# Products of single column tiles in other orders: a two-layer decoder trunk on one core

## The chip, the cores and the metric

The kernel runs on one core of one Trainium2 chip. The metric is the device time of one execution in microseconds (us); less is better. PE is the matmul engine, PEld its weight loads, DVE, ACT and POOL the vector, scalar and gpsimd engines, SP the engine that issues most transfers.

## The reference

A decoder trunk of two layers for 256 tokens of width 1024. Each layer has an attention mixer and a gated feed-forward with a causal convolution of width 3 on the gate branch; a last RMS norm ends it. The change lies in the feed-forward:

```python
def conv_ffn(h, w_in, conv_w, conv_b, w_out):
    u, g = jnp.split(h @ w_in, 2, axis=-1)
    g = lax.conv_general_dilated(g, conv_w[:, None, :], window_strides=(1,),
                                 padding=[(CONV_WIDTH - 1, 0)],
                                 dimension_numbers=('NWC', 'WIO', 'NWC'),
                                 feature_group_count=D_FF) + conv_b
    return (jax.nn.gelu(g, approximate=False) * u) @ w_out
...
    for layer in range(DEPTH):
...
        h = h + conv_ffn(rmsnorm(h, ffn_norm[layer]), ffn_w_in[layer], ffn_conv_w[layer],
                         ffn_conv_b[layer], ffn_w_out[layer])
    return rmsnorm(h, final_norm)
```

Here `h` is 256 by 1024, `w_in` 1024 by 5632 (2816 columns for u, 2816 for g) and `w_out` 2816 by 1024.

## The kernel before

Every float32 operand of a large product is held as two parts, a high part and the rest (`whi` and `wlo` of a weight, `xs[:, k, 0]` and `xs[:, k, 1]` of the activation). A product is three matmuls added into one PSUM region: high times high (hh), high weight times low activation (hl), low weight times high activation (lh). Weights come in chunks of 128 by 2048 in the order of a list (`PLAN`); ACT copies a chunk's high part (L145) and DVE subtracts it (L146), in two pieces of 1024 columns.

A feed-forward works through 22 column tiles `f` of 128 of the 2816. In a product of a tile, u (`i` = 0) and g (`i` = 1) each add up over eight blocks `k` of 128 of the width. The two banks are `pd`. Tiles 0 to 4 take the dense form (`colmajor`, three matmuls of 256 columns per block; u and g are the two halves of one bank, and change after every trio). Tiles 5 to 21 (`NARROW` = 5) take the wide form (`product`): one matmul of 512 columns gives hh and hl side by side in the two halves of a bank, a second of 256 columns adds lh to the first half. `read_out` then adds the halves: ACT copies the low half to `lowp` (L876), DVE adds it (L877). DVE scales u and g into `gbuf` (L900), ACT and DVE do the convolution, ACT the gelu, POOL the gating, ACT and DVE split the result into the parts `o`.

Four tiles later (`LAGF` = 4) `proj` multiplies `o` with two rows of blocks of `w_out` and adds into banks that stay open through the whole feed-forward (`acc`). In layer 0 (`proj_tile`) these are four banks, each with two 256-column regions `c`, and the weight is the stationary operand: 24 matmuls of 256 columns per tile, hh, hl, lh for each `c`. In layer 1 (`final`, `proj_tail`) the activation is the stationary operand and the weights stream: five regions in five banks (`TAIL`), 15 matmuls per tile.

PE's order is the program's order. On the other engines the order in this loop is written out by hand too: product of `f`, split of a chunk if `f` is even, gelu and split of `f-1`, read-out of `f`, split of the next chunk with the convolution, then `proj(f-4)`. PSUM has eight banks, shared by `acc` and `pd`.

Of the kernel before, what the change touches and what calls it, by code (L numbers as in the profile page):

```python
# [28 lines left out]
S = 256  # L29
D = 1024  # L30
KD = D // 128
# [19 lines left out]
TAIL = ((0, 0, 512), (0, 512, 1024), (1, 0, 512), (1, 512, 768), (1, 768, 1024))  # L51
# [50 lines left out]
def trunk(ctx, tc, x, rel_bias, small, lam_p, wpack, fin_g, onehot, addrow, tab, out):  # L102
    nc = tc.nc
# [11 lines left out]
    def bank(name="ps"):  # L115
        return psum.tile([128, 512], F32, name=name, tag="ps")

    def t2(name, dt=F32, shape=(128, 2, S)):
        return two.tile(list(shape), dt, name=name, tag="t2")

    def mm(o, l, r, start, stop):
        nc.tensor.matmul(o, l, r, start=start, stop=stop, skip_group_check=True)  # L122
# [83 lines left out]
    xs = xpool.tile([128, KD, 2, S], F32R, name="xs")  # L206
# [243 lines left out]
        return kt, [((('qn', h), ('kn', h), 'kr'), stage_s), ((), stage_t), (('vm',), stage_o)]  # L450


    def proj_tile(acc, o, w, kk, first, last):
        oh, ol = o
        hi, lo = w
        for c in range(KD):
            a = acc[c // 2][:, (c % 2) * S:(c % 2 + 1) * S]
            s = slice(c * 128, (c + 1) * 128)
            mm(a, hi[:, kk, s], oh, first and c % 2 == 0, False)
            mm(a, hi[:, kk, s], ol, False, False)  # L460
            mm(a, lo[:, kk, s], oh, False, last)

    def close_phase(acc, g0):
        for j in range(4):
# [26 lines left out]
    def bc2(t):  # L491
        return t[:, None, :].to_broadcast([128, 2, S])
# [52 lines left out]
    def proj_units(prefix, order, store):  # L545
        box = {}

        def unit(i):
            kt = order[i]

            def run():
                if i == 0:
                    box['acc'] = [bank("acc") for _ in range(4)]
                proj_tile(box['acc'], store[kt], need(f"{prefix}{kt // 2}"), kt % 2, i == 0, i == KD - 1)
            return kt, run
        return [unit(i) for i in range(KD)], box
# [181 lines left out]
    def ffn(l, final):  # L738
        env, acts, box = {}, {}, {}
# [5 lines left out]
        def conv(f):  # L745
            g = gbuf[f % 3][:, 1]
            t1 = work.tile([128, S], F32, name="t1", tag="sc")
            nc.scalar.activation(t1, g[:, 2:], AF.Identity, bias=col(f, 3), scale=col(f, 2))  # L748
            return t1

        def taps(f, t1):
            g = gbuf[f % 3][:, 1]
            t3 = work.tile([128, S], F32, name="t3", tag="pt", bufs=6)
            nc.vector.scalar_tensor_tensor(t3, g[:, 1:S + 1], col(f, 1), t1, op0=ALU.mult, op1=ALU.add)
            nc.vector.scalar_tensor_tensor(t3, g[:, 0:S], col(f, 0), t3, op0=ALU.mult, op1=ALU.add)
            return t3

        def gelu(f, t3):
            ge = work.tile([128, S], F32, name="ge", tag="ex", bufs=6)
            nc.scalar.activation(ge, t3, AF.Gelu)  # L760
            nc.gpsimd.tensor_tensor(ge, ge, gbuf[f % 3][:, 0, 2:], op=ALU.mult)  # L761
            return ge

        def act_split(f, ge):
            o = t2("o", F32R)
            nc.scalar.activation(o[:, 0], ge, AF.Copy)  # L766
            nc.vector.tensor_tensor(o[:, 1], ge, o[:, 0].bitcast(F32), op=ALU.subtract)  # L767
            acts[f] = (o[:, 0], o[:, 1])
# [15 lines left out]
        def weights(f):  # L784
            n = f"f{l}o{f // 2}"
            return need(n) if f < NARROW - LAGF or f >= NF - LAGF else chunks[n]

        def proj(f):
            w = weights(f)
            first, last = f == 0, f == NF - 1  # L790
            if first:
                box['acc'] = [bank("acc") for _ in range(len(TAIL) if final else 4)]
            if not final:
                proj_tile(box['acc'], acts[f], w, f % 2, first, last)
                return
            for i in range(len(TAIL)):
                proj_tail(f, i)

        def proj_tail(f, i):
            w = weights(f)  # L800
            (oh, ol), (hi, lo) = acts[f], w
            tb, c0, c1 = TAIL[i]
            a = box['acc'][i][:, :c1 - c0]
            s = slice(tb * 128, (tb + 1) * 128)
            mm(a, oh[:, s], hi[:, f % 2, c0:c1], f == 0, False)
            mm(a, ol[:, s], hi[:, f % 2, c0:c1], False, False)
            mm(a, oh[:, s], lo[:, f % 2, c0:c1], False, f == NF - 1)
# [28 lines left out]
        for f in range(3, NARROW):  # L836
            dense(f)
            if final:
                hn_tile()
                hn_tile()  # L840
            if f >= LAGF:
                proj(f - LAGF)
# [8 lines left out]
        def next_chunk():  # L851

            i = split_at[0]
            if i >= len(PLAN):
                return [lambda: None] * 2
            split_at[0] += 1
            ps = pieces(i)[1]

            def step(n):
                if n == 0:  # L860
                    open_split(i)
                if n < len(ps):
                    split_piece(i, ps[n])
                if n == 1:
                    load_next()
            return [lambda: step(0), lambda: step(1)]

        def product(f, i, p):
            hi, lo = chunks[f"f{l}i{f}"]
            for k in range(KD):  # L870
                mm(p, hi[:, 8 * i + k], xs[:, k], k == 0, False)
                mm(p[:, :S], lo[:, 8 * i + k], xs[:, k, 0], False, k == KD - 1)

        def read_out(t, i, p):
            lowp = work.tile([128, S], F32, name="lowp", tag="ex", bufs=6)
            nc.scalar.activation(lowp, p[:, S:], AF.Copy)  # L876
            nc.vector.tensor_tensor(t[:, i], p[:, :S], lowp, op=ALU.add)  # L877

        need(f"f{l}i{NARROW}")
        with tc.manual_schedule(engines={mybir.EngineType.Activation, mybir.EngineType.DVE,  # L880
                                         mybir.EngineType.Pool, mybir.EngineType.SP}):
            t3 = None
            for f in range(NARROW, NF):
                even = f % 2 == 0
                pu, pg = bank("pd"), bank("pd")
                product(f, 0, pu)
                product(f, 1, pg)
                if even:
                    c = next_chunk()
                    c[0]()  # L890
                if t3 is not None:
                    ge = gelu(f - 1, t3)
                if even:
                    c[1]()
                if t3 is not None:
                    act_split(f - 1, ge)
                ug = t2("ug")
                read_out(ug, 0, pu)
                read_out(ug, 1, pg)
                nc.vector.tensor_tensor(gbuf[f % 3][:, :, 2:], ug, bc2(env['r_bc']), op=ALU.mult)  # L900
                c = next_chunk()
                c[0]()
                t3 = taps(f, conv(f))
                c[1]()
                proj(f - LAGF)
            act_split(NF - 1, gelu(NF - 1, t3))
        if not final:
            for f in range(NF - LAGF, NF):
                proj(f)
            close_phase(box['acc'], NORM1[1])  # L910
            return
# [3 lines left out]
        def piece(t, tb, c0, c1):  # L915
            return t[2 * tb + c0 // 512][:, c0 % 512:c0 % 512 + c1 - c0]

        for i, (tb, c0, c1) in enumerate(TAIL):
            for f in range(NF - LAGF, NF):
                proj_tail(f, i)  # L920
            h, o = piece(hn, tb, c0, c1), piece(y, tb, c0, c1)
            q = i if tb == 0 else i - 2
            nc.vector.tensor_add(h, box['acc'][i][:, :c1 - c0], h)
            t = t2("fsq", shape=(128, c1 - c0))
# [6 lines left out]
            if c1 == D:  # L931
# [4 lines left out]
                for c in range(2):  # L936
                    o = y[2 * tb + c]
# [17 lines left out]
    first = [bank("pd"), bank("pd")]  # L955
# [30 lines left out]
    split_at[0] = 3  # L986
    even_layer()
    ffn(0, False)
    odd_layer()
    ffn(1, True)  # L990


# [68 lines left out]
```

## Time and profile before

| what | value |
|---|---|
| median of 3 runs | 606.71 us (605.46 to 606.84) |
| profiled execution, its time | 607.95 us |
| its span, first to last instruction | 606.1 us |
| PE busy | 591.7 us, 98% of the span, 4078 matmuls |
| PE weight loads | 4078 |
| DVE busy / ACT busy / POOL busy | 73% / 58% / 17% |
| granted PE clock, mean over the span | 0.993 |

The span is the profiled execution's time on the core; its own time has 1.85 us more around it. Matmuls overlap in the pipe, so PE's busy time is not the sum of separate matmuls; how fast they follow each other is read from the starts in the timeline and from the chain of work that ended last.

### The profile page before, as it was taken

How to read it: one execution, taken by the hardware profiler on the slowest of the kernel's cores; microseconds unless marked ns; L12 is line 12 of the kernel's file. 1: busy time of each engine (PE TensorE's matmuls, PEld its weight loads, DVE VectorE, ACT ScalarE, POOL GpSimd, SP SyncE). 2: the span in 40 equal slices, each digit the busy share in tenths (PEclk: the TensorE clock that was granted, in tenths of full speed). 3: DMA queues.
4: the chain of work that ended last, by engine and by line, in shares of the span. 5: the costliest groups of instructions: out<-in, count | busy, mean ns of one | idle time of the engine just before them, and what ended most of it. 6: DMA issues, size and time to landing. Idle time of an engine off the chain costs nothing.

```text
span 606.1 us, 10380 instructions
## 1 busy us (share of the span) xinstructions
PE 591.7 (98%) x4078; PEld 544.6 (90%) x4078; DVE 443.0 (73%) x778; ACT 351.6 (58%) x647; POOL 103.0 (17%) x97
## 2 busy tenths in 40 slices
PE   8998999999999999999999999999989999999995
PEld 7887989999999999999999998999978888888884
DVE  5698757679877778777786975558857787777754
ACT  6558557466655556565564755645655565655633
POOL 4701122041101111001144101004201111011110
PEclk8999999999999999999999999999989999999999
DMA  7988543435455554554435343454535545554301
GB/s 264 335 322 316 193 171 142 141 138 208 146 203 209 209 183 169 203 207 166 170 120 215 134 147 132 144 196 119 202 140 208 198 164 195 209 176 170 142 0 70
DMA packets 19961, 108.77 MB, mean 179 GB/s; under 512 B 2430, under 2 KB 5448, under 8 KB 7752
## 3 DMA queue, kind: packets, MB, share of 16 engines
q1 hardware_dynamic: 16416, 104.17, 47.4%
q10 hardware_dynamic: 3336, 3.41, 1.7%
q0 software_dynamic: 160, 0.52, 0.4%
q8 instruction: 32, 0.52, 0.4%
q14 instruction: 17, 0.14, 0.1%
HBM read 107.02 MB, written 1.08 MB: 178 GB/s over the span
## 4 chain that ended last, share of the span: by engine, by line
PE 84%; DVE 6%; DMA 4%; ACT 2%; issue 1%; POOL 1%; SPq 0%; POOLq 0%; ACTq 0%; DVEq 0%
PE pd L122 48%; PE acc L122 26%; PE pv L122 4%; DMA raw<-in_wpack_dram 3%; DVE wlo L146 3%; PE pO L122 2%; PE pS L122 2%; DMA hT<-in_x_dram 1%; PE puq L122 1%; DVE ex L341 1%; DVE sc L331 1%; ACT whi L145 1%; PE pukv L122 0%; POOL ge L761 0%; PE pT L345 0%
## 5 line engine op out<-in xcount | busy, mean ns | idle before, releaser
L122 PE MATMUL pd<-xs,whi 128*128 128x256 f32 (+1 forms) x1312 | 331.3, 332 | 3.7 <-ACT hn L833 2.2
L122 PE MATMUL pd<-xs,wlo 128*128 128x256 f32 x928 | 258.0, 283 | 0.4 <-DVE wlo L146 0.4
L146 DVE TENSOR_TENSOR wlo<-raw,whi 128x1024 fp32r<-128x1024 f32 (+1 forms) x183 | 229.3, 1278 | 26.4 <-ACT whi L145 26.2
L122 PEld LDWEIGHTS pd<-xs,whi 128*128 128x128 f32 x1312 | 221.0, 191 | 27.1 <-ACT whi L145 2.5
L145 ACT ACTIVATE whi<-raw 128x1024 fp32r<-128x1024 f32 (+1 forms) x195 | 196.4, 1032 | 69.4 <-PE pd L122 18.2
L122 PEld LDWEIGHTS pd<-xs,wlo 128*128 128x128 f32 x928 | 175.7, 192 | 0.8 <-DVE wlo L146 0.8
L122 PE MATMUL acc<-o,whi 128*128 128x256 f32 x608 | 108.7, 281 | 0.0
L122 PEld LDWEIGHTS acc<-o,whi 128*128 128x128 f32 x608 | 92.7, 188 | 1.0 <-issue 0.2
L761 POOL TENSOR_TENSOR ge<-ge,gbuf 128x256 f32<-128x256 f32 x44 | 37.4, 851 | 294.8 <-ACT ge L760 294.8
L122 PE MATMUL acc<-o,wlo 128*128 128x256 f32 x304 | 84.7, 279 | 0.0
L876 ACT ACTIVATE lowp<-pd 128x256 f32<-128x256 f32 x68 | 25.9, 381 | 81.2 <-PE pd L122 81.1
L877 DVE TENSOR_TENSOR ug<-pd,lowp 128x256 f32<-128x256 f32 x68 | 28.5, 419 | 52.7 <-ACT lowp L876 52.7
L122 PE MATMUL acc<-whi,o 128*128 128x512 f32 (+1 forms) x220 | 58.5, 351 | 0.2 <-ACT o L766 0.2
L122 PEld LDWEIGHTS acc<-o,wlo 128*128 128x128 f32 x304 | 57.2, 188 | 0.0
L122 PEld LDWEIGHTS acc<-whi,o 128*128 128x128 f32 x220 | 38.6, 189 | 7.5 <-ACT o L766 0.7
L146 POOL TENSOR_TENSOR wlo<-raw,whi 128x1024 fp32r<-128x1024 f32 (+1 forms) x12 | 26.3, 2192 | 104.2 <-ACT whi L145 58.0
L122 PE MATMUL acc<-wlo,o 128*128 128x512 f32 (+1 forms) x110 | 38.6, 351 | 0.0
L767 DVE TENSOR_TENSOR o<-ge,o 128x256 fp32r<-128x256 f32 x44 | 19.0, 438 | 22.1 <-ACT o L766 22.1
L748 ACT ACTIVATE t<-gbuf,ccol 128x256 f32<-128x256 f32 x44 | 26.4, 601 | 12.0 <-DVE gbuf L900 10.1
L766 ACT ACTIVATE o<-ge 128x256 fp32r<-128x256 f32 x44 | 18.4, 418 | 24.0 <-POOL ge L761 24.0
L334 ACT ACTIVATE ex<-sc,nm 128x256 f32<-128x256 f32 (+1 forms) x56 | 24.8, 444 | 9.6 <-DVE nm L331 9.4
L122 PE MATMUL pv<-whi,xs 128*128 128x512 f32 x96 | 30.2, 395 | 0.0
(152 smaller groups left out, 536.5 us busy)
## 6 DMA issues: line engine op xcount, KB each, us to landing
raw<-in_wpack_dram SPq DMA_DIRECT2D x95, 1024.0 KB, 4.8
raw<-in_wpack_dram SPq DMA_DIRECT2D x8, 256.0 KB, 4.6
Tt<-btab ACTq DMA_DIRECT2D x2, 1024.0 KB, 9.2
hT<-in_x_dram SPq DMA_DIRECT2D x4, 256.0 KB, 5.1
Tt<-btab ACTq DMA_DIRECT2D x1, 512.0 KB
raw<-in_wpack_dram SPq DMA_DIRECT2D x1, 512.0 KB
fin<-in_fin_g_dram POOLq DMA_DIRECT2D x2, 256.0 KB, 4.0
out_dram<-y SPq DMA_DIRECT2D x2, 256.0 KB, 2.0
```

Source lines behind the costliest of these rows:

```text
L122: nc.tensor.matmul(o, l, r, start=start, stop=stop, skip_group_check=True)
L145: nc.scalar.activation(hi[:, s], raw[:, s], AF.Copy)
L146: (eng or nc.vector).tensor_tensor(lo[:, s], raw[:, s], hi[:, s].bitcast(F32), op=ALU.subtract)
L331: nc.vector.tensor_tensor_reduce(out=t[:, a:b], in0=p[:, a:b], in1=rev(T, b - a), scale=-1.0, scalar=BIG, op0=ALU.add, op1=ALU.min, accum_ ...
L334: nc.scalar.activation(e[:, a:b], t[:, a:b], AF.Exp, bias=nm[:, i:i + 1], scale=-1.0, accum_out=den[:, i:i + 1])
L341: nc.vector.tensor_scalar(e[:, a:b], e[:, a:b], rd[:, i:i + 1], None, op0=ALU.mult)
L748: nc.scalar.activation(t1, g[:, 2:], AF.Identity, bias=col(f, 3), scale=col(f, 2))
L761: nc.gpsimd.tensor_tensor(ge, ge, gbuf[f % 3][:, 0, 2:], op=ALU.mult)
L766: nc.scalar.activation(o[:, 0], ge, AF.Copy)
L767: nc.vector.tensor_tensor(o[:, 1], ge, o[:, 0].bitcast(F32), op=ALU.subtract)
L876: nc.scalar.activation(lowp, p[:, S:], AF.Copy)
L877: nc.vector.tensor_tensor(t[:, i], p[:, :S], lowp, op=ALU.add)
```

## The change

In layer 0, tiles 5 to 9 keep the wide form with its two matmuls per block, in another order for tiles 6, 7 and 8. Tiles 10 to 16 leave the wide form for three matmuls of 256 columns into one half bank, in seven different orders. For them `read_out` is one DVE copy per bank and `lowp` is gone. The output products of tiles 5 to 9 in layer 0 go through their 24 matmuls in five other orders. In layer 1 only the output products of tiles 6 and 7 change their order; all else there is as before.

```diff
-    def proj_tile(acc, o, w, kk, first, last):
+    def proj_tile(acc, o, w, kk, first, last, order='triple'):
         oh, ol = o
         hi, lo = w
-        for c in range(KD):
+        three = ('hh', 'hl', 'lh')
+        seq = {'triple': [(c, x) for c in range(KD) for x in three],
+               'banks': [(c, x) for c in (0, 2, 4, 6, 1, 3, 5, 7) for x in three],
+               'pairs': [(c + i, x) for c in range(0, KD, 2) for x in three for i in range(2)],
+               'passes': [(c, x) for x in three for c in (0, 2, 4, 6, 1, 3, 5, 7)],
+               'hlh': [(c, x) for c in range(KD) for x in ('hh', 'lh', 'hl')],
+               'across': [(c + i, x) for c in (0, 1, 4, 5) for x in three for i in (0, 2)]}[order]
+        for c, x in seq:
...
+                order = {5: 'banks', 6: 'pairs', 7: 'passes', 8: 'hlh', 9: 'across'}.get(f, 'triple')
...
+            for tb in range(2) if f in (6, 7) else ():
+                (oh, ol), (hi, lo) = acts[f], w
+                s = slice(tb * 128, (tb + 1) * 128)
+                its = [(box['acc'][i][:, :c1 - c0], slice(c0, c1)) for i, (t, c0, c1) in enumerate(TAIL) if t == tb]
+                for a, c in its:
+                    if f == 6:
+                        mm(a, oh[:, s], hi[:, f % 2, c], False, False)
+                    else:
+                        mm(a, oh[:, s], hi[:, f % 2, c], False, False)
+                        mm(a, oh[:, s], lo[:, f % 2, c], False, False)
+                for a, c in its:
+                    mm(a, ol[:, s], hi[:, f % 2, c], False, False)
+                for a, c in its if f == 6 else ():
+                    mm(a, oh[:, s], lo[:, f % 2, c], False, False)
...
-        def product(f, i, p):
+        WIDE = {5: 'kpair', 6: 'kswap', 7: 'passes', 8: 'ug', 9: 'kpair'}
+        NARROW3 = {10: 'triple', 11: 'passes', 12: 'ug', 13: 'hlh', 14: 'lhh', 15: 'ugtriple', 16: 'ugk'}
+
+        def products(f, ps):
...
+            total = KD * (3 if f in NARROW3 and not final else 2)
...
+            order = 'kpair' if final else WIDE.get(f) or NARROW3.get(f) or 'kpair'
+            if total == 2 * KD:
+                seq = {'kpair': [(i, k, w) for i in range(2) for k in range(KD) for w in ('wide', 'lh')],
+                       'kswap': [(i, k, w) for i in range(2) for k in range(KD)
+                                 for w in (('wide', 'lh') if k % 2 == 0 else ('lh', 'wide'))],
+                       'passes': [(i, k, w) for i in range(2) for w in ('wide', 'lh') for k in range(KD)],
+                       'ug': [(i, k, w) for k in range(KD) for w in ('wide', 'lh') for i in range(2)]}[order]
+            else:
+                three, rot = ('hh', 'hl', 'lh'), ('hh', 'lh', 'hl')
+                seq = {'triple': [(i, k, w) for i in range(2) for k in range(KD) for w in three],
+                       'passes': [(i, k, w) for i in range(2) for w in three for k in range(KD)],
+                       'ug': [(i, k, w) for k in range(KD) for w in three for i in range(2)],
+                       'hlh': [(i, k, w) for i in range(2) for k in range(KD) for w in rot],
+                       'lhh': [(i, k, w) for i in range(2) for k in range(KD) for w in ('lh', 'hl', 'hh')],
+                       'ugtriple': [(i, k, w) for k in range(KD) for i in range(2) for w in three],
+                       'ugk': [(i, k, w) for w in three for k in range(KD) for i in range(2)]}[order]
...
+        def read_out(t, i, p, f):
+            if f in NARROW3 and not final:
+                nc.vector.tensor_copy(t[:, i], p[:, :S])
+                return
             lowp = work.tile([128, S], F32, name="lowp", tag="ex", bufs=6)
             nc.scalar.activation(lowp, p[:, S:], AF.Copy)
             nc.vector.tensor_tensor(t[:, i], p[:, :S], lowp, op=ALU.add)
```

PE, the start of the product of tile 10 of layer 0, before the change (`pd` are u's and g's banks, `whi` and `wlo` the parts of the weight, `xs` the activation):

```order
L122 MATMUL pd<-xs,whi 128x512
L122 MATMUL pd<-xs,wlo 128x256
L122 MATMUL pd<-xs,whi 128x512
L122 MATMUL pd<-xs,wlo 128x256
L122 MATMUL pd<-xs,whi 128x512
```

The same place with the change:

```order
L122 MATMUL pd<-xs,whi 128x256 x2
L122 MATMUL pd<-xs,wlo 128x256
L122 MATMUL pd<-xs,whi 128x256 x2
L122 MATMUL pd<-xs,wlo 128x256
L122 MATMUL pd<-xs,whi 128x256 x2
```

Each 512-column matmul has become two of 256, so a tile has 48 matmuls and 48 weight loads where it had 32 of each.

PE with the change, from tile 11's product (`passes`) over the output product of tile 7 (`acc`, `passes`) into tile 12's product (`ug`):

```order
L122 MATMUL pd<-xs,whi 128x256 x16
L122 MATMUL pd<-xs,wlo 128x256 x8
L122 MATMUL pd<-xs,whi 128x256 x16
L122 MATMUL pd<-xs,wlo 128x256 x8
L122 MATMUL acc<-o,whi 128x256 x16
L122 MATMUL acc<-o,wlo 128x256 x8
L122 MATMUL pd<-xs,whi 128x256 x4
L122 MATMUL pd<-xs,wlo 128x256 x2
```

Before, tile 11 was 16 pairs of 512 and 256 columns and the output product eight trios, and u was finished before g began; now the kinds stand in blocks, and in tile 12 u and g alternate after every matmul, so that both banks are finished only at the end.

DVE, the read-out of one of the tiles 10 to 16, before the change (`ug` is the tile that is scaled into `gbuf`, `wlo` the split of a weight chunk):

```order
L877 TENSOR_TENSOR ug<-pd,lowp 128x256 x2
L900 TENSOR_TENSOR gbuf_122<-ug,r_bc 128x2x256
L146 TENSOR_TENSOR wlo<-raw,whi 128x1024
L754 SCALAR_TENSOR_TENSOR t_2880<-gbuf_122,ccol_308,t_2878 128x256
L755 SCALAR_TENSOR_TENSOR t_2880<-gbuf_122,ccol_308,t_2880 128x256
```

The same place with the change:

```order
L926 COPY ug<-pd 128x256 x2
L952 TENSOR_TENSOR gbuf_122<-ug,r_bc 128x2x256
L146 TENSOR_TENSOR wlo<-raw,whi 128x1024
L760 SCALAR_TENSOR_TENSOR t_2952<-gbuf_122,ccol_308,t_2950 128x256
L761 SCALAR_TENSOR_TENSOR t_2952<-gbuf_122,ccol_308,t_2952 128x256
```

The two additions have become two copies, which no longer come after ACT's `lowp`; the rows around them stand in the same order.

## Rows read from the trace of the kernel before

**Rows 1.** The page's busy time, share of the span and instructions of each engine.

```profile
PE 591.7 (98%) x4078; PEld 544.6 (90%) x4078; DVE 443.0 (73%) x778; ACT 351.6 (58%) x647; POOL 103.0 (17%) x97
```

**Rows 2.** Chain that ended last, 120 to 320 us: start, us, what.

```profile
122.45 11.52 PE pd L122 x96
...
140.59 11.51 PE pd L122 x96
152.10 2.83 PE acc L122 x24
...
163.40 5.56 PE pd L122 x32
168.96 2.83 PE acc L122 x24
171.78 5.55 PE pd L122 x32
...
196.92 5.55 PE pd L122 x32
...
247.20 5.55 PE pd L122 x32
...
294.66 14.13 PE acc L122 x120
```

**Rows 3.** Busy time of each engine in two stretches (feed-forward loops of the two layers).

```profile
152.00:294.70 142.70, 142.70 (x955) 131.36 (x955) 107.69 (x154) 82.19 (x136) 15.20 (x18) 1.00 0.53 191
...
446.70:590.00 143.30, 143.28 (x792) 124.60 (x792) 103.96 (x149) 80.11 (x134) 14.07 (x17) 0.99 0.44 159
```

**Rows 4.** Timeline of PE at the program's start, by-kind order of matmuls.

```profile
17.06 1.12 PE L122 MATMUL pd<-xs,wlo 128*128 128x256 f32 x8
18.02 2.08 PE L122 MATMUL pd<-xs,whi 128*128 128x256 f32 x16
19.94 1.12 PE L122 MATMUL pd<-xs,wlo 128*128 128x256 f32 x8
20.90 0.40 PE L122 MATMUL pd<-xs,whi 128*128 128x256 f32 x2
```

**Rows 5.** Timeline of PE and PEld at 160 us: an output product of layer 0.

```profile
160.66 0.28 PE L122 MATMUL acc<-o,wlo 128*128 128x256 f32 x1
...
160.78 0.40 PE L122 MATMUL acc<-o,whi 128*128 128x256 f32 x2
160.90 0.19 PEld L122 LDWEIGHTS acc<-o,wlo 128*128 128x128 f32 x1
...
161.01 0.28 PE L122 MATMUL acc<-o,wlo 128*128 128x256 f32 x1
...
161.13 0.40 PE L122 MATMUL acc<-o,whi 128*128 128x256 f32 x2
```

**Rows 6.** Timeline of DVE after one product of layer 0.

```profile
161.10 0.43 DVE L877 TENSOR_TENSOR ug<-pd,lowp 128x256 f32<-128x256 f32 x1 [0.85 <-ACT lowp L876]
...
164.22 3.93 DVE L146 TENSOR_TENSOR wlo<-raw,whi 128x1024 fp32r<-128x1024 f32 x3
```

**Rows 7.** Timeline of PE in an output product of layer 1.

```profile
578.74 0.40 PE L122 MATMUL acc<-whi,o 128*128 128x256 f32 x2
578.97 0.29 PE L122 MATMUL acc<-wlo,o 128*128 128x256 f32 x1
579.10 0.40 PE L122 MATMUL acc<-whi,o 128*128 128x256 f32 x2
579.33 0.28 PE L122 MATMUL acc<-wlo,o 128*128 128x256 f32 x1
```

**Rows 8.** Chain that ended last, whole span: a stretch of 512-column matmuls.

```profile
83.12 5.47 PE pv L122 x24
```

**Rows 9.** Read-out instructions: by line on the page, and by tile (min/median/max ns).

```profile
L876 ACT ACTIVATE lowp<-pd 128x256 f32<-128x256 f32 x68 | 25.9, 381 | 81.2 <-PE pd L122 81.1
L877 DVE TENSOR_TENSOR ug<-pd,lowp x68: 406/423/427, 159.8 to 585.7; 128x256 f32<-128x256 f32 x68
L264 DVE COPY r_bc<-psb x4: 409/417/424, 29.4 to 425.8; 128x256 f32<-128x256 f32 x4
```

**Rows 10.** Weight loads by line and shape: busy us, mean ns of one, idle before.

```profile
L122 PEld LDWEIGHTS pd<-xs,whi 128*128 128x128 f32 x1312 | 221.0, 191 | 27.1 <-ACT whi L145 2.5 <-ACT hn L833 2.5 <-issue 0.3
```

## What the change is predicted to do, and why

> **What bounds the kernel now.** I read the page's busy times first [rows 1]: PE is busy 98% of the span and every other engine has room. The second view was the chain of work that ended last [rows 2]. From 152 us to the end of the layer-0 feed-forward it names nothing but PE: each tile is a product of 32 matmuls in 5.55 us and an output product of 24 in 2.83 us, one behind the other (tile 6 starts at 163.40 us, tile 7 at 171.78, tile 10 at 196.92, tile 16 at 247.20). The busy times by stretch say the same [rows 3]: in that loop PE is busy for all 142.70 us, at a granted clock of 1.00, the upper of its two levels (2.4 GHz), while DVE has 35 us to spare and ACT 60. In the loop of layer 1 it is 143.28 of 143.30 us. So in the stretches that the change touches, time is the number of matmuls by their spacing, and nothing else decides unless a wait appears.
>
> **The spacing by kind.** A wide pair (512 columns and 256) takes 5.55 / 16 = 0.347 us [rows 2]. Three matmuls of 256 columns on the same operands, in the dense form, take 3 × 11.51 / 96 = 0.360 us [rows 2]. Three in an output product take 3 × 2.83 / 24 = 0.354 us [rows 2]. So the trio streams as many columns as the pair, and costs 7 to 13 ns more.
>
> **Tiles 10 to 16, pair to trio.** Seven tiles with 16 blocks (eight each of u and g) lose 16 matmuls of 512 and gain 32 of 256: 112 matmuls and 112 weight loads more in all. By the dense rows a tile goes from 5.55 to 48 × 0.1199 = 5.755 us, +0.205; seven tiles are +1.4 us. By the output product's rows it is 48 × 0.1179 = 5.66, +0.11; seven are +0.8 us. I take +1.4, since the dense rows have the same stationary and moving tiles; both ends go into the range.
>
> **The seven orders among them.** The trace has two orders of such trios on the same operands. At the start of the program the matmuls stand by kind, and change the region after every two: from 17.06 to 18.02 us 8 of them take 0.96 us, from 18.02 to 19.94 us 16 take 1.92 [rows 4], 0.120 us each. The dense form (hh, hl, lh of one block) has 0.1199 [rows 2]. The two orders cost the same, so I give the other orders the same price. A matmul beside one with the same weight gets no discount: there are as many loads as matmuls [rows 1], although the dense and the output products put hh and hl with one weight side by side.
>
> The Trainium skill ("TensorE: Matmul & The Clock Gate", section "Step-by-step: what each phase is for") says that loading is apart from multiplying so that a weight can be loaded once and used repeatedly. The page's loads, as many as its matmuls, show that this program does not use that, so grouping by weight saves no load.
>
> **Wide tiles 6, 7 and 8 and the output products.** The numbers of matmuls and columns stay. Bounds for a matmul of 256 columns: the fastest spacing per column is that of 24 matmuls of 512 columns in 5.47 us [rows 8], 0.228 each or 0.114 per 256; the slowest is the 0.120 of the dense form. The output products lie at 0.118. For 5 × 24 matmuls that is −0.5 to +0.3 us, for the three wide tiles and layer 1's two output products less than half of that. I take 0.
>
> **Read-outs.** Fourteen `lowp` copies of ACT (0.381 us each) vanish, fourteen DVE additions of 0.423 us become copies, for which the nearest row is a copy out of PSUM of 0.417 us [rows 9]. Neither is on the chain, so I price it at nothing; PE's own work covers it. Without that cover it would be worth at most 14 × 0.381 = 5.3 us, but no wait of PE in the loop could give it back. In tiles 8, 12, 15 and 16 u is finished only with g, so the DVE row that scales into `gbuf`, and what stands behind it there (a chunk's split, the convolution), come one read-out (0.42 us) later. That is covered: in the trace the read-out that starts at 161.10 us ends at 161.53, and the banks are next needed by the product two tiles on, at 171.78 [rows 2, 6]; the splits queued behind end at 168.15 us (164.22 + 3.93), 3.6 us before the same product. Where u and g alternate, the second half of a chunk is needed at the product's start instead of 2.8 us later; the splits end before the start.
>
> **The sum.** +1.4 (trios) + 0 (orders) + 0 (read-outs) = +1.4 us. The profiled execution, 607.95 us, would be 609.4; it stands 1.2 us above the median of the three runs, so the same sum on the median, 606.71, gives 608.1 us, +0.23%. About 0.3% (1.8 us) is what a measurement of this kernel can tell from no change.
>
> **Rivals.**
> *Changing the bank costs time.* In an output product of layer 1 two matmuls in one bank start 0.115 us apart (578.74 to 578.97), the one that leaves the bank takes 0.13 (578.97 to 579.10) [rows 7]: 15 ns. The change makes some 205 more changes of bank (about 48 each in tiles 12 and 16, 48 in tiles 8 and 15, 48 in output products 7 and 9, the rest in `banks` and layer 1). With 15 ns each it is +3.1 us on top of 1.4: 611.2 us, slower. It decides from 2 ns a change (0.4 us / 205). Against it: in layer 0 the step to the other half of a bank (160.66 to 160.78) and the step to another bank (161.01 to 161.13) both take 0.12 us [rows 5], and 16 matmuls of the by-kind start, with several changes, take no more than 0.120 each [rows 4]. Chance 0.16.
>
> *Weight loads come into the open.* If a load could not run under a matmul, 112 more of 0.191 us [rows 10] would be +21 us: 628 us. Against it: matmuls 0.12 us apart each have a load of 0.19 us that starts while the one before is running [rows 5]. A trio is already paced like this, so it would take something that only the new orders do. Chance 0.04. The Trainium skill speaks for it ("TensorE: Matmul & The Clock Gate", section "The mechanism"): a load overlaps a running matmul only where the row groups differ, and here all matmuls use all 128 rows. The trace's loads under matmuls do not agree. With that page's 128 / 1.2 = 107 ns a load ("LDWEIGHTS (loading the stationary operand)") the estimate would be +12 us.
>
> *The order loosens the spacing.* If the 0.120 comes from adding into the same region again and again, alternating would bring it to the 0.114 of [rows 8]: seven tiles at 48 × 0.114 = 5.47 us are −0.6, the five output products −0.5, together 605.7 us. Against it: the by-kind start alternates regions and keeps 0.120 [rows 4]. Chance 0.08; even so it barely reaches a measurable gain.
>
> *A late read-out holds PE.* It needs a delay of over 3.6 us in DVE's queue, and I find 0.42. It would cost what goes over, in four tiles: with 1 us each, 612 us. Chance 0.02.
>
> **How the numbers follow.** The forecast, +0.8 to +1.4 us with some tenths for the orders, has 0.70: 607.2 to 608.4, and as the median of a few runs moves by 0.7 us either way, 606.5 to 609.1. The range takes in the gain at the lower end and part of the bank rival at the upper: 605.6 to 609.9. Slower by over 0.3%: 0.14 of the bank rival, 0.04 of the loads, 0.02 of the read-out and 0.04 of the forecast's upper edge, 0.24. Faster: 0.03 of the third rival. The rest, 0.73, is within 0.3%.
>
> **What would show it.** In the profile after, PE should have 4190 matmuls and as many loads, ACT 633 instructions. In the chain the products of tiles 10 to 16 should read 48 matmuls in 5.66 to 5.76 us whatever their order, the wide ones 5.55, the output products 2.83, and PE's busy time should still fill the loop. Wrong would be: tiles that differ among themselves by more than 0.1 us (then order matters), a tile of 5.5 us or less, an idle time of PE ahead of a `pd` or `acc` row, or a load that no longer starts under the matmul before it.

## The result, and the profile after

The changed kernel took 609.55 us (median of 3 runs, 609.32 to 610.11) against 606.71 us: 1.0051 times the time before, 95% interval 1.0028 to 1.0074. In twelve more runs, beside 29 of the kernel before, it was 1.0020 (1.0004 to 1.0036), medians 608.43 and 606.54 us. The two intervals overlap between 1.0028 and 1.0036. Three runs far off the rest are left out of every ratio: 825.9 and 968.7 us of the kernel before and 1132.2 us of the trios alone, at a mean granted clock of 0.655, 0.557 and 0.921. The profiled executions agree with the larger set: the span is 607.7 us, 1.6 more than before.

The page's busy times after; they answer to [rows 1]:

```profile
PE 592.7 (98%) x4190; PEld 549.4 (90%) x4190; DVE 442.3 (73%) x778; ACT 347.6 (57%) x633; POOL 103.5 (17%) x97
```

There are 112 matmuls and 112 loads more, 14 ACT instructions fewer, and as many on DVE as before. PE's busy time grew by 1.0 us and says little, since matmuls overlap. The chain that ended last (start, us, what) is the view to read against [rows 2]:

```profile
152.00 2.83 PE acc L122 x24
...
163.29 5.58 PE pd L122 x32
...
171.68 5.58 PE pd L122 x32
...
188.47 5.56 PE pd L122 x32
...
196.85 5.75 PE pd L122 x48
202.61 2.83 PE acc L122 x24
205.44 5.75 PE pd L122 x48
211.19 2.83 PE acc L122 x24
214.03 5.75 PE pd L122 x48
...
222.61 5.75 PE pd L122 x48
...
231.20 5.75 PE pd L122 x48
...
239.79 5.75 PE pd L122 x48
...
248.37 5.75 PE pd L122 x48
...
256.96 5.65 PE pd L122 x32
...
296.12 14.13 PE acc L122 x120
310.25 11.51 PE pd L122 x96
```

The reader is to see three things. The seven products of 48 matmuls, in seven orders, take 5.75 us each. The reordered wide products of tiles 6 and 7 (163.29 and 171.68; tile 8 is like them) take 5.58 instead of 5.55 or 5.56. The first wide product behind the trios, at 256.96, takes 5.65. From 152.00 to 310.25 is 158.25 us; before, from 152.10 to the end of the 14.13 us row that starts at 294.66, it was 156.69 [rows 2]. So the whole difference of the spans, 1.6 us, lies in this loop. There PE is still never idle (the busy times of the stretch; they answer to [rows 3]):

```profile
152.00:310.20 158.20, 158.20 (x1185) 151.29 (x1185) 118.51 (x168) 87.18 (x135) 18.82 (x20) 1.00 0.52 187
```

### The profile page after: what moved, and what is told of

Same layout as the page of the kernel before. It is cut to its first block, busy times and chain, and to the rows that moved or that the text cites. A ratio compares the mean times of both kernels' runs of the same rounds, so it can differ in the third digit from the quotient of the medians.

```text
span 607.7 us, 10570 instructions
## 1 busy us (share of the span) xinstructions
PE 592.7 (98%) x4190; PEld 549.4 (90%) x4190; DVE 442.3 (73%) x778; ACT 347.6 (57%) x633; POOL 103.5 (17%) x97
## 4 chain that ended last, share of the span: by engine, by line
PE 84%; DMA 5%; DVE 4%; ACT 2%; issue 2%; POOL 1%; SPq 0%; POOLq 0%; ACTq 0%; DVEq 0%
PE pd L122 48%; PE acc L122 26%; PE pv L122 4%; DMA Tt<-btab 2%; DMA raw<-in_wpack_dram 2%; PE pO L122 2%; PE pS L122 2%; DVE wlo L146 2%; DMA hT<-in_x_dram 1%; PE puq L122 1%; DVE ex L341 1%; PE pukv L122 0%; ACT whi L145 0%; DVE sc L331 0%; POOL ge L767 0%
## 5 line engine op out<-in xcount | busy, mean ns | idle before, releaser
L122 PE MATMUL pd<-xs,whi 128*128 128x256 f32 (+1 forms) x1424 | 325.7, 319 | 3.2 <-ACT hn L854 2.2
L122 PEld LDWEIGHTS pd<-xs,whi 128*128 128x128 f32 x1424 | 230.5, 191 | 21.3 <-ACT hn L854 2.5
L122 PE MATMUL pd<-xs,wlo 128*128 128x256 f32 x928 | 246.9, 283 | 0.9 <-DVE wlo L146 0.7
L122 PEld LDWEIGHTS pd<-xs,wlo 128*128 128x128 f32 x928 | 171.8, 191 | 3.0 <-DVE wlo L146 1.5
L122 PE MATMUL acc<-o,whi 128*128 128x256 f32 x608 | 107.2, 281 | 0.0
L122 PE MATMUL acc<-o,wlo 128*128 128x256 f32 x304 | 82.4, 279 | 0.0
L929 ACT ACTIVATE lowp<-pd 128x256 f32<-128x256 f32 x54 | 20.3, 379 | 64.9 <-PE pd L122 64.9
L930 DVE TENSOR_TENSOR ug<-pd,lowp 128x256 f32<-128x256 f32 x54 | 22.6, 421 | 43.5 <-ACT lowp L929 43.4
```

## The experiments

Ratios are to the kernel before, run on the same chip beside each. The runs stood on three chips, where the kernel before had medians of 606.54, 606.98 and 606.98 us, so two runs of different chips are compared by their ratios or with these medians in mind. Lines of the diffs are against the changed kernel unless another is named.

### The same kernel again

> The changed kernel once more, in more rounds beside the kernel before. The two profiles differ by 1.6 us in span (606.1 and 607.7), the medians by 2.8. By the price of a matmul (trio 0.360 us, pair 0.347) the ratio is 1.0026 (+1.4 to +1.6 us) and the 2.8 is the spread of the few runs. By a cost that the profiled execution does not show, the ratio stays at 1.0047.

Measured: 1.0020 (1.0004 to 1.0036), span 607.6 us. That is +1.2 us by the ratio (0.2 to 2.2) and 1.9 by the medians. The interval holds the price of the matmuls, 1.4 to 1.6 us, and not 2.8.

### The orders alone

```diff
-        NARROW3 = {10: 'triple', 11: 'passes', 12: 'ug', 13: 'hlh', 14: 'lhh', 15: 'ugtriple', 16: 'ugk'}
+        NARROW3 = {}
```

> The new orders of the wide tiles 6 to 8 and of the output products, but no trios: tiles 10 to 16 stay wide. By the price of a matmul nothing changes in number: +0.0 us (within 0.2 us), wide products 5.55 to 5.58 us. If a change of bank has a price of 15 ns, about 95 more changes give +1.4 us.

Measured: 0.9995 (0.9981 to 1.0009), medians 606.71 and 606.54 us. The orders of the wide tiles and of the output products cost nothing that can be measured; 15 ns a change of bank (1.0023) is outside the interval.

### The trios alone

```diff
-        WIDE = {5: 'kpair', 6: 'kswap', 7: 'passes', 8: 'ug', 9: 'kpair'}
-        NARROW3 = {10: 'triple', 11: 'passes', 12: 'ug', 13: 'hlh', 14: 'lhh', 15: 'ugtriple', 16: 'ugk'}
+        WIDE = {}
+        NARROW3 = {f: 'triple' for f in range(10, 17)}
...
-                order = {5: 'banks', 6: 'pairs', 7: 'passes', 8: 'hlh', 9: 'across'}.get(f, 'triple')
+                order = 'triple'
...
-            for tb in range(2) if f in (6, 7) else ():
+            for tb in ():
...
-            for i in range(len(TAIL)) if f not in (6, 7) else ():
+            for i in range(len(TAIL)):
```

> Tiles 10 to 16 of layer 0 as trios, all in the order hh, hl, lh, everything else in the order of before. By the price of a matmul the whole loss is here: +1.4 to +1.6 us, each of the seven products 5.75 us. If the orders carry the loss, under +1 us.

Measured: 1.0024 (1.0009 to 1.0040), +1.5 us, and each of the seven products 5.75 us, the second of them:

```profile
206.03 5.75 PE pd L122 x48
```

Within the noise the whole loss is here, and the order of the trios adds nothing that can be measured.

### All tiles as trios

The same with `range(5, 22)`, and `final` no longer excepted in `products` and `read_out`.

> All 17 tiles from 5 to 21 as trios in the order hh, hl, lh, in both layers: 34 tiles in place of 7. By the price of a matmul 34 x 0.205 = +7.0 us (613.7 on a median of 606.7). If a trio cost more than its profile shows (the 2.8 us of the medians for seven tiles), +13.6 us. If the ACT copies that vanish gave something back, under +5 us.

Measured: 1.0092 (1.0072 to 1.0112), +5.6 us by the ratio, 6.45 by the medians. In layer 0 a product is 5.75 us (chain):

```profile
206.50 5.75 PE pd L122 x48
212.25 2.83 PE acc L122 x24
```

The expected 7.0 us (34 x 0.205) lies a little above the interval, 4.4 to 6.8 us. Row by row the chain gives 6.4: 16 tiles of layer 0 lose 0.20 us each, its tile 5, which took 5.65 before, loses 0.10, and the 17 products of layer 1, 5.74 or 5.75 us against 5.56, lose 0.18 to 0.19 each. The loss grows with the number of trios, and 14 or 68 vanished ACT copies give nothing back that shows.

### Fewer columns, the same loads

From all trios, hl with half its columns (it leaves out hl for half of the tokens):

```diff
-                mm(ps[i][:, :S * (2 if what == 'wide' else 1)], w[:, 8 * i + k], a, done[i] == 1,
-                   done[i] == total)
+                cw = S // 2 if what == 'hl' else S * (2 if what == 'wide' else 1)
+                if what == 'hl':
+                    a = xs[:, k, 1, :cw]
+                mm(ps[i][:, :cw], w[:, 8 * i + k], a, done[i] == 1, done[i] == total)
```

> All 34 tiles as trios as in the run with all trios (+5.6 to +6.5 us), but every hl matmul has 128 columns in place of 256: the low part of the activation is left out for half of the tokens in these products. 544 matmuls lose 128 columns and keep their weight load. If each matmul has a fixed price of 13 ns on top of its columns (256 more columns cost 107 ns), an hl matmul goes from 0.120 to 0.067 us: 29 us less than with all trios, about 584 us. If a matmul of 256 is paced by its weight load, nothing is gained: 0.110 to 0.120 us stays, 607 to 613 us.

Measured: 607.43 us, 1.0006 (0.9985 to 1.0028): 5.2 us less than all trios by the ratios, not 29. Chain and then timeline of PE, layer 0:

```profile
205.36 5.58 PE pd L122 x48
210.94 2.80 PE acc L122 x24
```

```profile
197.86 0.34 PE L122 MATMUL pd<-xs,whi 128*128 128x256 f32 x2
198.04 0.33 PE L122 MATMUL pd<-xs,wlo 128*128 128x256 f32 x1
198.21 0.34 PE L122 MATMUL pd<-xs,whi 128*128 128x256 f32 x2
```

A block takes 5.58 / 16 = 0.349 us for 640 columns, where the trio had 0.360 for 768 and the pair has 0.347 for 768. From the start of hh to that of lh, behind the short hl, it is 0.18 us; but from lh to the next hh it is 0.17 us, not 0.12. My theory of a fixed price of 13 ns on top of the columns falls: by it the block would have lost some 53 ns, and it lost 11. While three full loads stay, a block of fewer columns still takes 0.349 / 3 = 0.116 us a load.

### Fewer columns and a smaller load

On top of the last edit, hl also uses half of its weight columns, so half of the tile's outputs get no hl:

```diff
-                mm(ps[i][:, :cw], w[:, 8 * i + k], a, done[i] == 1, done[i] == total)
+                m = 64 if what == 'hl' else 128
+                mm(ps[i][:m, :cw], w[:, 8 * i + k, :m], a, done[i] == 1, done[i] == total)
```

> As the run with hl of 128 columns, and its weight load is halved too: 64 of 128 weight columns (this leaves out hl for half of the tile's outputs as well). The three matmuls of a block took 0.349 us there, 0.116 a load. If the columns that are loaded set the pace, the block falls by most of half a load, to about 0.31 us: a product 4.9 to 5.1 us and the whole some 18 us less than with hl128. If each load and matmul has a fixed beat of 0.116 us whatever its size, the product stays at 5.58 us and the time at 606 to 608 us.

Measured: 0.9974 (0.9955 to 0.9994), 605.25 us. The chain:

```profile
204.18 5.55 PE pd L122 x48
209.72 2.80 PE acc L122 x24
```

A block takes 0.347 us and not 0.31: my expectation missed. The expectation of a fixed beat (5.58 us, 606 to 608 us) came closer. One reading is that the edit was badly placed. Timeline of PE and PEld:

```profile
198.56 0.22 PE L122 MATMUL pd<-xs,whi 128*64 128x128 f32 x1
198.57 0.19 PEld L122 LDWEIGHTS pd<-xs,wlo 128*128 128x128 f32 x1
198.62 0.33 PE L122 MATMUL pd<-xs,wlo 128*128 128x256 f32 x1
```

What starts beside the short hl is the load of lh, and that one is still whole; the load of hl, which got smaller, stands beside hh with its 256 columns. By its row lh starts 0.06 us behind hl all the same, but takes 0.33 us instead of 0.28. That the full load holds it there is argued, not shown.

### The smaller load alone

The same edit with hl's full 256 columns; half of the tile's outputs get no hl.

> All 34 tiles as trios, hl with its full 256 columns, but a weight load of 64 columns (hl is left out for half of the tile's outputs). If a matmul of 256 is held by the load ahead of it, the load of hl no longer holds its neighbour and the block falls from 0.360 toward the pair's 0.347: 7 us less than all trios, the time of before. If the columns streamed hold it, it stays at 0.360 (5.75 us a product, 612 to 613 us).

Measured: 1.0020 (1.0002 to 1.0037), 607.57 us; all trios were at 1.0092. The chain, and the loads of the loop by shape (count, busy us, mean ns):

```profile
205.24 5.61 PE pd L122 x48
210.84 2.81 PE acc L122 x24
```

```profile
L122 PEld LDWEIGHTS pd<-xs,whi 128*128 128x128 f32 x259 | 48.6, 188 | 0.0
...
L122 PEld LDWEIGHTS pd<-xs,whi 128*64 128x64 f32 x259 | 35.4, 137 | 0.0
```

The block streams as many columns as a full trio and takes 5.61 / 16 = 0.351 us instead of 0.360. One load that is 51 ns shorter gives back 9 of the 13 ns by which a trio exceeds a pair. So the surcharge does not go by the number of columns, which is 768 in all three forms; most of it goes when one of three loads is halved. The edit also halves what that matmul writes (64 rows of the bank, not 128), and no run parts this from the load.

### All trios, the bank changed after every matmul

From all trios:

```diff
-        NARROW3 = {f: 'triple' for f in range(5, 22)}
+        NARROW3 = {f: 'ug' for f in range(5, 22)}
```

> All 34 tiles as trios, but u and g alternate after every matmul, so the bank changes 47 times a tile and not once; both banks end together. By the price of a matmul the same as all trios in the plain order, +5.6 to +6.5 us, and 5.75 us a tile. If a change of bank costs 15 ns, 1,560 more changes are +23 us on top; if it costs 2 ns, +3 us. A read-out that comes too late would show as idle PE ahead of pd.

Measured: 1.0153 (1.0125 to 1.0181), 3.7 us over all trios by the ratios. The chain in layer 0, and the timeline of PE at the first alternating product of layer 1:

```profile
204.92 5.75 PE pd L122 x48
210.67 2.83 PE acc L122 x24
```

```profile
443.51 0.28 PE L122 MATMUL pd<-xs,whi 128*128 128x256 f32 x1
448.61 1.01 PE L122 MATMUL pd<-xs,whi 128*128 128x256 f32 x3 [4.82 <-ACT hn L854]
```

Some 1,560 more changes of bank cost nothing in the loops: 5.75 us is the same product. The loss is at one wait, which with all trios in the plain order was 2.09 us: after u's first matmul the first of g waits 4.82 us until ACT has emptied g's bank of `hn`. In the order of before u's whole product comes first, and its 2.8 us lie under that wait. The wait is 2.73 us longer. Behind it the granted clock stood at 0.50 from 448 to 452 us, and the rest of the product took 8.03 us; the profiled execution of all trios kept 1.00 there. That the clock makes up the rest of the 3.7 us fits, and was not parted from the wait.

### All wide tiles and output products alternating

```diff
-        WIDE = {5: 'kpair', 6: 'kswap', 7: 'passes', 8: 'ug', 9: 'kpair'}
-        NARROW3 = {10: 'triple', 11: 'passes', 12: 'ug', 13: 'hlh', 14: 'lhh', 15: 'ugtriple', 16: 'ugk'}
+        WIDE = {f: 'ug' for f in range(5, 22)}
+        NARROW3 = {}
...
-            order = 'kpair' if final else WIDE.get(f) or NARROW3.get(f) or 'kpair'
+            order = WIDE.get(f) or NARROW3.get(f) or 'kpair'
...
-                order = {5: 'banks', 6: 'pairs', 7: 'passes', 8: 'hlh', 9: 'across'}.get(f, 'triple')
+                order = 'across'
```

> No trios. All 34 wide tiles with u and g alternating after every matmul, and the output products of layer 0 (all tiles) changing the bank after every matmul. By the price of a matmul no change, +0.0 us; from the profile of the changed kernel up to +0.03 us a product (5.58 for 5.55) and -0.03 us an output product, +0.5 us in all. With 15 ns a change of bank, some 1,400 changes are +21 us.

Measured: 1.0065 (1.0041 to 1.0088), +4 us, where at most +0.5 was expected. The chain:

```profile
205.25 5.59 PE pd L122 x32
210.84 2.80 PE acc L122 x24
```

A product and its output product take 8.39 us where they took 8.38: the order is free in the loop here too. Again PE waits 4.72 us on `hn` at the start of layer 1's loop; the next two runs tell whether that is the loss.

### The same in layer 0 only

The last kernel with the `final` case back in `kpair`.

> Of the run with all wide tiles in the alternating order only layer 0's part (17 wide tiles with u and g alternating, all output products changing the bank after every matmul); layer 1 as before. If a bank that is late at the start of layer 1 made the loss there, nothing is left: +0.0 to +0.5 us. If the 700 changes of bank cost, +2 us or more (half of the +4).

Measured: 1.0012 (0.9995 to 1.0028), medians 607.01 and 606.98 us. +2 us is outside the interval, though layer 0 holds some 950 of the changes of bank (17 x 30 and 22 x 20), more than the 700 that I had counted. The loss of the last kernel was in layer 1. The chain, in layer 0 and at g's half of the first product of layer 1's loop (used at the end):

```profile
203.57 5.59 PE pd L122 x32
209.16 2.80 PE acc L122 x24
...
445.51 3.04 PE pd L122 x16
```

### One product in the alternating order

All wide, output products as before, and

```diff
-            order = 'kpair' if final else WIDE.get(f) or NARROW3.get(f) or 'kpair'
+            order = 'ug' if final and f == 5 else 'kpair'
```

> The kernel before with one single product in the alternating order: tile 5 of layer 1, the first after the dense tiles. g's bank there comes free only when ACT has read the transposed residual out of it, and in the order of before the 2.8 us of u's product run under that wait. If that wait is the whole loss of the alternating runs, +2.4 to +2.8 us from this one tile, with PE idle 4.8 us ahead of the second matmul. If the loss is spread over the changes of bank, +0.0 us.

Measured: 1.0076 (1.0062 to 1.0091), +4.6 us by the ratio, +3.65 us by the medians. One reordered product of 34 costs more than the seven tiles of trios. The timeline row of PE, and the granted clock (third number from the right) in the stretches behind it:

```profile
445.93 0.79 PE L122 MATMUL pd<-xs,whi 128*128 128x512 f32 x1 [4.72 <-ACT hn L854]
```

```profile
444.00:446.00 2.00, 0.07 (x1) 0.07 (x1) 0.43 (x1) 1.25 (x4) 0.64 (x1) 0.92 0.66 197
446.00:448.00 2.00, 2.00 (x6) 1.71 (x7) 0.00 (x0) 0.37 (x1) 0.00 (x0) 0.50 0.78 328
448.00:450.00 2.00, 2.00 (x11) 1.72 (x10) 0.00 (x0) 0.00 (x0) 0.00 (x0) 0.73 0.00 0
```

The wait is 4.72 us, 2.56 more than the 2.16 of the kernel before. That was expected, but the time grew by more than the 2.4 to 2.8 us expected of it. This fits the clock, which stands at its lower level behind the wait. All six runs had a mean granted clock of 0.991 or 0.996; beside those runs of the kernel before that had 0.993 to 0.996 on this chip, the means differ by 3.0 us (610.56 and 607.53).

### The pairs everywhere

From the kernel before, the dense tiles 0 to 4 made wide too:

```diff
+        def wide(fs, ps):
+            ws = [need(f"f{l}i{f}") for f in fs]
+            for k in range(KD):
+                for (hi, lo), pp in zip(ws, ps):
+                    for i, p in enumerate(pp):
+                        mm(p, hi[:, 8 * i + k], xs[:, k], k == 0, False)
+                        mm(p[:, :S], lo[:, 8 * i + k], xs[:, k, 0], False, k == KD - 1)
...
         def dense(f):
-            p = bank("pd")
-            colmajor(ug_items(p, f))
+            p = bank("pd"), bank("pd")
+            wide((f,), (p,))
             gate(f, p)
```

> The other way round, from the kernel before: the dense tiles 0 to 4 of both layers become wide pairs as well, so ten tiles lose 16 matmuls each; their read-outs get 20 more ACT copies and DVE additions. By the price of a matmul 10 x 0.205 = -2.0 us, 604.5 us on a median of 606.5. If the read-outs at the start of a layer, where PE waits for gelu and the splits, are late by as much, no gain or a loss of up to 2 us.

Measured: 1.0246 (1.0217 to 1.0275), 622.34 us. The chain, in place of 11.51 us and 96 matmuls a pair of tiles, and what PE waited for:

```profile
122.83 11.36 PE pd L122 x64
```

```profile
PE acc L122 <- DVE ug L788: 6.2, 2, 4.9
PE pd L122 <- DVE ug L788: 4.0, 1, 4.0
PE acc L122 <- ACT hn L844: 2.3, 1, 2.3
PE pd L122 <- DVE wlo L146: 1.8, 2, 1.6
```

A pair of dense tiles gains 0.15 us, where the price of a trio had promised 0.41; a block of the wide form takes 11.36 / 32 = 0.355 us here, not 0.347. And each tile now holds two banks until its read-out: PE waits over 10 us for `ug`, the read-out that empties them. The mean granted clock of the execution was 0.979, against 0.993. The version that the price of a trio pointed to is the slowest of all.

## Why the prediction held, step by step

*What bounds the kernel.* Right: the loop's time is PE's matmuls by their spacing, before and after.

*Pair to trio.* Right in the step and its size: +0.205 us a tile from the dense rows, measured 5.75 - 5.55 = 0.20, seven times 1.4 us. Why a trio costs more than a pair on equal columns the prediction did not say, and below it stays open. The lower bound, from the output products, was not reached by any order.

*The seven orders.* Right, and more widely than the two rows of before could say: all seven products took 5.75 us. Over all 34 tiles two of the orders gave the same product time.

*Wide tiles and output products at 0.* Mis-sized by a little: the four wide tiles 6 to 9 measured about +0.1 us together, and the first wide product after the trios +0.10, which I had not in the sum. Tile 5 behind the dense form has the same 5.65 us in both kernels; what makes a first wide product slower was not tried. In layer 1 the product behind tile 7's reordered output product took 5.64 us instead of 5.56, in both traces of the changed kernel; its cause is open too. The output products gave back some hundredths. So the loop grew by 1.56 us where I had 1.4.

*Read-outs at nothing.* Right here: PE has no idle time in the loop.

*The sum on the median.* 608.1 us was predicted; the larger set has 608.43, the first three runs 609.55. Those three lie outside the 606.5 to 609.1 that had a chance of 0.70, and their +0.5% is in the class (slower by over 0.3%) that had 0.24. They lie inside the range only because its upper edge was widened for the bank rival, which fell; that part was luck. Part of the gap is the clock: all three had a mean granted clock of 0.995 or 0.996. Of the later twelve, six had 0.991 to 0.996 and took 608.35 to 611.39 us; the six with 0.998 or 0.999 took 606.42 to 608.51. Beside runs of the kernel before with the like clock, the twelve are 2.3 us longer on average in the first group and 1.4 in the second; the trios alone are 2.2 and 1.8. Whether the true loss is 0.2 or 0.3% the runs leave open; both intervals hold 0.28 to 0.36%, the spans say 0.26%.

*The rivals.* The bank rival fell: 1,560 more changes of bank left a product at 5.75 us, and the 15 ns of [rows 7] is no price of a change of bank in layer 1 either. There tile 6's output product now changes the bank after nearly every matmul, and takes the 2.81 us of before:

```profile
494.61 2.81 PE acc L122 x15
```

The loosened spacing fell with it: no order of trios was below 5.75 us. The loads in the open fell as I had sized it (0.191 us each, +21 us). It may have held a part: a load starts under the matmul before it, and yet a block was 9 ns shorter with one load halved. The late read-out did not come in this change; its like came where I had not looked, in the first product of layer 1, once the alternating order was put there.

What makes the 13 ns is not shown. It is not the number of columns, which pair and trio share. Most of it went with either of two changes: a sixth fewer columns gave back 11 ns a block, a halved load (with that matmul's halved outputs) at equal columns 9 ns. Columns alone would have given 53 ns in the first case, loads alone nothing. That a load runs beside the matmul ahead of it, and holds the next one when it is the longer of the two, fits the three runs with 128 columns or 64 weight columns to within 5 ns a block (an estimate, from the 0.114 us of 256 columns in [rows 8] and 0.116 us a full load); it was argued from them. It does not say why three full loads take 0.120 us each in the trio and 0.116 beside the short hl. A beat of some 0.116 us a matmul, whatever its load and columns, would give nearly the same blocks (0.348 against 0.349, 0.347 and 0.351), and leaves the trio's 0.360 open as well. A kernel with the short load beside the short matmul, which would part the two, was not run.

## What to carry to other kernels

Price a matmul by the spacing of the nearest stream on the same operands, not by its columns: here three matmuls of 256 columns took 0.360 us, and one of 512 with one of 256 took 0.347 for the same 768 columns. So fewer and wider matmuls won a little, and the order among them nothing inside the loop. Carried to all 34 tiles the price held within a tenth (6.4 of 7.0 us); carried to the dense tiles it gave 0.15 of 0.41 us. Before interleaving two accumulations, ask when the second one's bank comes free: a whole product in front of it may be what hides the wait. And a form that holds two banks where one did can cost more in waits for banks (over 10 us here) than its matmuls win.

## What was not expected of the hardware

At the start of layer 1's loop PE waits for `hn` in every version, and the granted clock behind that wait differs from one execution to another. The kernel before, with 2.16 us idle at 446.72 (columns as above, the clock third from the right):

```profile
446.00:448.00 2.00, 1.28 (x7) 1.15 (x8) 0.85 (x2) 1.43 (x4) 0.00 (x0) 1.00 0.88 356
448.00:450.00 2.00, 2.00 (x8) 1.69 (x7) 0.00 (x0) 0.00 (x0) 0.00 (x0) 0.51 0.13 53
450.00:452.00 2.00, 2.00 (x8) 1.66 (x7) 0.37 (x1) 0.78 (x2) 0.00 (x0) 0.64 0.04 8
```

All trios, with 2.09 us idle at 450.20:

```profile
450.00:452.00 2.00, 1.80 (x15) 1.80 (x16) 0.45 (x2) 0.63 (x2) 0.00 (x0) 1.00 0.86 360
452.00:454.00 2.00, 2.00 (x16) 1.87 (x15) 0.60 (x2) 0.75 (x1) 0.00 (x0) 1.00 0.00 0
```

One stands at 0.51 (the lower level) for the better part of 4 us, the other stays at 1.00. The chain of the kernel before has g's half of that product as

```profile
446.72 4.40 PE pd L122 x16
```

and the kernel that alternates in layer 0 alone, whose clock stayed up, has the same 16 matmuls in 3.04 us: about 1.4 us, as much as the whole change costs. Of the ten executions profiled with a wait of 2.1 to 2.2 us there, the clock fell in seven and stayed in three (all trios, the trios alone, and the alternation in layer 0 alone); with 4.7 to 4.8 us it fell in all three. The seven had a mean granted clock of 0.993 to 0.996 over the span, the three 0.997 to 0.999, so in these executions the mean tells the two apart. So single runs of this kernel scatter by more than the effect under study, and a profiled execution must be compared with one of the same clock at this place; those of the kernel before and the changed one both had the lower clock there.
